# A hybrid decoder step: four queue places on VectorE in an already tuned kernel

## The chip, the core and the metric

The kernel runs on one core of a Trainium2 chip. A core has five engines with a queue of instructions each: TensorE (PE, matrix multiply into PSUM), VectorE (DVE), ScalarE (ACT), GpSimd (POOL) and SyncE (SP). An engine takes its instructions in the order of its queue and waits, where one needs it, on the result of another engine or on a DMA transfer; what is queued behind a waiting instruction waits with it. The metric is the time of one execution on the device in microseconds (us); lower is better.

## The reference, cut

One inference step through two trunk layers of width 1024: 16 meta tokens and 1024 prompt tokens as one sequence, and 8 sequences that decode one token each. Everything is float32.

```python
# layer 0: h += conformer_conv(rmsnorm(h));  h += mlp(rmsnorm(h))
# layer 1: h += rwkv7(rmsnorm(h));           h += mlp(rmsnorm(h));  then a final rmsnorm
def _sqrelu_mlp(h, w_in, w_out):                       # 1024 -> 4096 -> 1024
    return jnp.square(jax.nn.relu(h @ w_in)) @ w_out

def _rwkv7(h, shift_prev, S0, ...):
    prev = concatenate([shift_prev[:, None, :], h[:, :-1]], axis=1)
    xx = prev - h                                      # the token-shift difference
    xr, xw, xk, xv, xa, xg = (h + xx * x_mix[i] for i in range(6))
    r, k, v = xr @ w_r, xk @ w_k, xv @ w_v
    decay = exp(-exp(-softplus(-(w0 + tanh(xw @ w1) @ w2)) - 0.5))
    a = sigmoid(a0 + (xa @ a1) @ a2);  g = sigmoid(xg @ g1) @ g2
    ...
    S_final, ys = lax.scan(_wkv7_step, S0, xs)         # 16 heads, 64 x 64 states
    ...                                                # group norm, bonus
    return ((yn + bonus) * g) @ w_o, h[:, -1], S_final

def _wkv7_step(S, inp):
    sa = einsum('bhvk,bhk->bhv', S, -kk_t)
    S = S * w_t + sa * (kk_t * a_t) + v_t * k_t
    return S, einsum('bhvk,bhk->bhv', S, r_t)
```

## The kernel before, in words

Activations lie with the 1024 channels on the partitions, as 8 tiles of 128 (KT = 8), and tokens along the free side. Each dense product is made of three matmuls of rounded halves (helper lines L190, L191, L192: high by high, high by the weight's low half, low by high). The low halves come from a subtraction at L142 (VectorE, tiles hl, z_l) or L165 (GpSimd, wo_lo, wi_lo), the high ones from a cast on ScalarE (L141, L158). The projections of RWKV (L909) use plain float32.

The MLP runs over 32 blocks of the hidden 4096: `ps_in` is the product into the block, VectorE applies the norm's factor at L347, ScalarE the ReLU at L348, L141 and L142 split it into `hh` and `hl`, and `out` collects the products back, which VectorE adds onto `h` at L360. VectorE's reading of `ps_in` for `hl` frees its PSUM bank.

Layer 0 handles the tokens in three groups (G0). Layer 1 handles them in two ways:

- The projections are made in four groups (G1). `prepare(g)` loads the normed tokens `hx` from DRAM and makes `xx` = previous token minus token, eight subtractions (L873) of which k = 2 and k = 5 go to GpSimd and six to VectorE; group 3 has one more for the 8 decode tokens (L878). `mix` makes the mixed inputs `mx` (L883). For each pair of heads the keyed factors follow: `rk`, `wa` (a scan of the log decays at L1122, then L1141, L1142, L1144), ScalarE's exponentials `em`, `ex`, and the products `ab` at L1153 and L1154.
- The recurrence runs over 17 chunks. Each chunk needs the inverse of a small triangular matrix. `inverses(c, n)` makes them for n chunks at once, five times in all (from chunks 0, 1, 5, 9 and 13): it loads the strictly triangular part `n` into `ni` from DRAM, runs up to 30 pairs of a product `tt` (L1208) and a sum `ni` (L1209) on VectorE, and stores the result, which `chunk` loads as `p` (L1240 transposes it, L1309 makes block copies of it). `nmask` (L774, L775) is the mask by which `n` is cut out of its product; it needs the load `m_ar`. In a chunk, `A` (L1246), `W`, `U`, `S` and `Y` are TensorE's products, `nr` and `xa` VectorE's copies of A, `fs` and `sv` VectorE's update of the state.

The later chunks run as fillers between the steps of the output projection (`mixer_out`, tiles z_h, z_l, ps_oo) and of the MLP of layer 1's first group. `decode_step` does the 8 decode tokens: four TensorE transposes (`pdd`), a store of six vectors to DRAM (`d_dec`), their load by heads (`dq`), then 16 slices of the state with products `t` (L1444), `sa`, `Sdec`, and the result `yd`, stored and reloaded as `eyd`, whose group norm begins with the sum `emsd` (L1469).

What sets the order: the program is written as interleaved generators (each `yield` gives a credit to the next), and a scheduler orders each engine's queue from its own model of durations, except where the source fixes it. In the RWKV part and layer 1 TensorE's order is the order in which it is written (`in_order`). Two calls fix places on other engines: `kept_place(x)` keeps an instruction in the order in which it is written, and

```python
with tc.issue_after(ins):
    ...
```

puts the instructions of its block that run on the engine of `ins` behind `ins` in that queue. It adds no wait of its own. `marks["hl2"][j]` is the split hl of MLP block j of layer 0's last group.

Of the kernel before, what the change touches and what calls it, by code (L numbers as in the profile page):

```python
# [12 lines left out]
ALU = mybir.AluOpType  # L13
# [3 lines left out]
P = 128  # L17
# [17 lines left out]
CHUNKS = [(1, 4), (5, 4), (9, 4), (13, 4)]  # L35
# [11 lines left out]
def hybrid_step(tc, x_prompt, x_sample, state_conv, state_shift, state_wkv, meta_tokens,  # L47
# [10 lines left out]
    with ctx:  # L58
# [715 lines left out]
        nc.vector.tensor_scalar(nmask, m_ar[:, :32], par32[:, 0:1], None, op0=ALU.mult)  # L774
# [59 lines left out]
        prep, norm, kept, scans = {}, {}, {}, {}  # L834
# [22 lines left out]
        def prepare(g):  # L857
# [13 lines left out]
            for k in range(KT):  # L871
                with nullcontext() if g else tc.issue_after(marks["hl2"][k + 5]):
                    first = (nc.gpsimd if k % 3 == 2 else nc.vector).tensor_sub(xx[:, k, :npr], hx[:, k, 0:npr], hx[:, k, 1:1 + npr])  # L873
                if g and k in (0, 2):
                    kept_place(first)
                yield
            if npr < n:
                nc.vector.tensor_sub(xx[:, :, npr:n], sps, hx[:, :, 1 + npr:1 + n])  # L878
# [65 lines left out]
        def mixer_in(g, tick):  # L944
# [140 lines left out]
            for p in range(KT):  # L1085
# [61 lines left out]
                for s in segs:  # L1147
                    e = ex[:, s[4]:s[4] + s[2], :s[3]]
                    e = bass.AP(e.tensor, e.offset, [*e.ap[:2], (1, 2), e.ap[2]])
                    two = lambda t: t[:, :, s[1]:s[1] + s[2] * s[3]].rearrange("p i (c t) -> p c i t", t=s[3])  # L1150
                    out = lambda i: ab[:, s[4]:s[4] + s[2], i:i + 2, :s[3]]

                    nc.vector.tensor_mul(out(0), two(rk2), e)  # L1153
                    nc.vector.tensor_mul(out(2), two(wa[:, :2, :]), cols(em, s).unsqueeze(2).broadcast_to([P, s[2], 2, s[3]]))  # L1154
# [33 lines left out]
        def inverses(c, n):  # L1188
# [8 lines left out]
            group = next((g for g in range(4) if CHUNKS[g][0] > max(c, 1)), None)  # L1197
            while group and group not in scans:
                yield 1
# [3 lines left out]
            for j in range(top - 2, 0, -1):  # L1203
# [3 lines left out]
                with tc.issue_after(scans[group]) if group and j == top - 2 else nullcontext():  # L1207
                    nc.vector.tensor_mul(o, ni[:, :j, j:j + 1].broadcast_to([B, j, wd]), ni[:, j:j + 1, j + 1:top].broadcast_to([B, j, wd]))  # L1208
# [206 lines left out]
        def decode_step():  # L1415

            with ExitStack() as s:
# [12 lines left out]
                yield 6  # L1430
# [149 lines left out]
        with ExitStack() as l1:  # L1580
# [15 lines left out]
            def mixer_out(g, actp, fill, add):  # L1596
# [5 lines left out]
                for p in range(0, KT, per):  # L1602
# [6 lines left out]
                    for i in range(some):  # L1609
                        split(z[0][p + i][:, :n], z[1][p + i][:, :n], v[:, i], nc.vector)  # L1610
# [72 lines left out]
            DL, DN, NL = 74, 90, 16  # L1683
# [75 lines left out]
```

## Time and profile before

| | |
|---|---|
| runs | 2680.71, 2673.79, 2672.78 us |
| median | 2673.79 us |
| profiled execution | 2680.24 us, its span 2678.5 us |
| mean granted TensorE clock | 0.991 |
| busy: TensorE | 2602.9 us (97%) |
| busy: VectorE | 1725.7 us (64%) |
| busy: ScalarE | 1132.7 us (42%) |
| busy: GpSimd | 1450.9 us (54%) |

A row of the timeline gives the start in us from the span's start, the duration in us, the engine, the source line, the operation, output and inputs by name, shapes, and in brackets the idle time of that engine just before it with what ended it. Adjacent instructions of one kind are put together (x8). Buffer numbers are left out of names. A row of a table by stretch gives the stretch, its length, the busy time of TensorE, its weight loads, VectorE, ScalarE and GpSimd with their counts, then the granted clock (1.00 is full speed), the share of the DMA engines and GB/s.

### The profile page before, as it was taken

Reading aid. Unit: us, or ns where it says so; the run is one execution under the profiler, and the core shown is the slowest. Engines: PE = TensorE matmul, PEld = TensorE weight load, DVE = VectorE, ACT = ScalarE, POOL = GpSimd, SP = SyncE. Lnnn points to the kernel's source line nnn. Section 1 sums busy time; section 2 is a strip of 40 time slices with the busy share of each in tenths; the row PEclk is TensorE's granted clock in tenths of the full one; section 3 lists DMA queues with packets and bytes.
Section 4 is the critical chain, followed back from the end, with each engine's and each line's share of the span. In section 5 each row is a group of like instructions: output and inputs, shape, how many; then the busy total and the mean of one; then the engine's idle time right before and its main releaser. Section 6 shows DMA issues by size and latency. Waiting matters only on the chain.

```text
span 2678.5 us, 51360 instructions
## 1 busy us (share of the span) xinstructions
PE 2602.9 (97%) x19796; PEld 2450.6 (91%) x19796; DVE 1725.7 (64%) x3584; ACT 1132.7 (42%) x2097; POOL 1450.9 (54%) x2060
## 2 busy tenths in 40 slices
PE   9999999999999999999899999899999999999998
PEld 8999999999998999877777887689999999999998
DVE  6999999997445444444857567686679643344435
ACT  5546445444444333333344445545443542222223
POOL 7677878878877776122211113375578763333331
PEclk9999999999999999999999999999999999999999
DMA  6663544554456443668766867897666542222211
GB/s 188 176 168 104 167 141 132 158 177 134 142 154 183 124 138 113 201 188 211 188 181 180 206 168 193 209 211 179 156 204 176 155 131 71 64 71 71 67 52 44
DMA packets 602058, 400.20 MB, mean 149 GB/s; under 512 B 96128, under 2 KB 548928, under 8 KB 601814
## 3 DMA queue, kind: packets, MB, share of 16 engines
q1 hardware_dynamic: 573764, 360.08, 49.1%
q0 software_dynamic: 8720, 26.35, 3.1%
q10 hardware_dynamic: 19330, 10.49, 1.4%
q8 instruction: 156, 2.56, 0.4%
q14 instruction: 88, 0.72, 0.1%
HBM read 338.94 MB, written 58.83 MB: 149 GB/s over the span
## 4 chain that ended last, share of the span: by engine, by line
PE 79%; DVE 11%; DMA 3%; ACT 2%; issue 2%; POOL 2%; SPq 0%; ACTq 0%; DVEq 0%; POOLq 0%
PE out L190 8%; PE ps_in L190 8%; PE ps_in L192 8%; PE ps_in L191 8%; PE out L191 8%; PE out L192 8%; PE pk L909 4%; PE pr L909 3%; PE pv L909 2%; DVE tt L1208 1%; DVE ni L1209 1%; PE ps_g L190 1%; PE ps_o L192 1%; PE ps_g L191 1%; PE ps_g L192 1%
## 5 line engine op out<-in xcount | busy, mean ns | idle before, releaser
L165 POOL TENSOR_TENSOR wo_lo<-wo_raw,wo_hi 128x256 fp32r<-128x256 f32 x736 | 539.3, 765 | 290.0 <-ACT wo_hi L158 281.0
L165 POOL TENSOR_TENSOR wi_lo<-wi_raw,wi_hi 128x256 fp32r<-128x256 f32 x640 | 474.7, 774 | 250.5 <-ACT wi_hi L158 249.8
L190 PE MATMUL out<-hh,wo_hi 128*128 128x352 f32 (+2 forms) x1536 | 499.8, 325 | 14.9 <-DVE hl L142 10.2
L360 DVE TENSOR_TENSOR h<-h,out 128x352 f32<-128x352 f32 (+2 forms) x768 | 386.9, 512 | 169.7 <-PE out L192 168.0
L190 PE MATMUL ps_in<-m_h,wi_hi 128*128 128x352 f32 (+2 forms) x1536 | 495.3, 322 | 0.0
L192 PE MATMUL ps_in<-m_l,wi_hi 128*128 128x352 f32 (+2 forms) x1536 | 494.2, 322 | 1.1 <-DVE m_l L288 1.1
L191 PE MATMUL out<-hh,wo_lo 128*128 128x352 f32 (+2 forms) x1536 | 494.5, 322 | 0.0
L191 PE MATMUL ps_in<-m_h,wi_lo 128*128 128x352 f32 (+2 forms) x1536 | 492.9, 321 | 0.0
L192 PE MATMUL out<-hl,wo_hi 128*128 128x352 f32 (+2 forms) x1536 | 492.8, 321 | 0.0
L542 DVE SCALAR_TENSOR_TENSOR cv<-u,wdw,cv 128x348 f32<-128x348 f32 (+2 forms) x720 | 378.4, 577 | 0.7
L158 ACT CAST wi_hi<-wi_raw 128x1024 fp32r<-128x1024 f32 x160 | 167.6, 1049 | 398.1 <-PE out L192 199.0
L158 ACT CAST wo_hi<-wo_raw 128x1024 fp32r<-128x1024 f32 x184 | 192.7, 1048 | 318.3 <-PE out L192 169.9
L190 PEld LDWEIGHTS out<-hh,wo_hi 128*128 128x128 f32 x1536 | 291.0, 189 | 21.1 <-DVE hl L142 11.5
L192 PEld LDWEIGHTS ps_in<-m_l,wi_hi 128*128 128x128 f32 x1536 | 289.2, 188 | 2.6 <-DVE m_l L288 2.1
L190 PEld LDWEIGHTS ps_in<-m_h,wi_hi 128*128 128x128 f32 x1536 | 290.3, 189 | 1.4
L191 PEld LDWEIGHTS out<-hh,wo_lo 128*128 128x128 f32 x1536 | 290.1, 189 | 0.8
L191 PEld LDWEIGHTS ps_in<-m_h,wi_lo 128*128 128x128 f32 x1536 | 289.5, 188 | 0.6
L192 PEld LDWEIGHTS out<-hl,wo_hi 128*128 128x128 f32 x1536 | 289.8, 189 | 0.0
L347 DVE SCALAR_TENSOR_TENSOR ps_in<-ps_in,rs_m 128x352 f32<-128x352 f32 (+2 forms) x192 | 100.6, 525 | 258.1 <-PE ps_in L192 257.8
L142 DVE TENSOR_TENSOR hl<-ps_in,hh 128x352 fp32r<-128x352 f32 (+2 forms) x192 | 98.7, 515 | 125.2 <-ACT hh L141 125.2
L1074 POOL DMA_DIRECT2D d_n<-n x32 | 24.3, 760 | 217.5 <-DVE n L1064 112.4
L348 ACT ACTIVATE ps_in<-ps_in 128x352 f32<-128x352 f32 (+2 forms) x192 | 85.1, 444 | 125.2 <-DVE ps_in L347 124.8
(367 smaller groups left out, 4770.1 us busy)
## 6 DMA issues: line engine op xcount, KB each, us to landing
wi_raw<-in_w_mlp_in_dram SPq DMA_DIRECT2D x160, 512.0 KB
wo_raw<-in_w_mlp_out_dram SPq DMA_DIRECT2D x160, 512.0 KB
wk_raw<-in_rwkv_w_k_dram SPq DMA_DIRECT2D x32, 512.0 KB
wr_raw<-in_rwkv_w_r_dram SPq DMA_DIRECT2D x32, 512.0 KB
wv_raw<-in_rwkv_w_v_dram SPq DMA_DIRECT2D x32, 512.0 KB
d_ab<-ab POOLq DMA_DIRECT2D x32, 512.0 KB, 4.5
pg_raw<-in_conv_w_pw_dram SPq DMA_DIRECT2D x24, 512.0 KB
pa_raw<-in_conv_w_pw_dram SPq DMA_DIRECT2D x24, 512.0 KB
```

What stands on the lines that cost most here:

```text
L142: return eng_lo.tensor_sub(lo, src, hi.bitcast(F32))
L158: cast = nc.scalar.copy(hi[:, :a * b], raw[:, :a * b])
L165: eng_lo.tensor_sub(lo[:, cs], raw[:, cs], hi[:, cs].bitcast(F32))
L190: nc.tensor.matmul(ps, w[0], act[0], start=first, stop=False)
L191: nc.tensor.matmul(ps, w[1], act[0], start=False, stop=False)
L192: nc.tensor.matmul(ps, w[0], act[1], start=False, stop=last)
L347: nc.vector.scalar_tensor_tensor(s, s, 0.0, rs()[:, :n], op0=ALU.max, op1=ALU.mult)
L348: nc.scalar.activation(s, s, AF.Square)
L360: total = nc.vector.tensor_add(hv[:, 4 * i + m, :], hv[:, 4 * i + m, :], ps[:, :n])
L542: nc.vector.scalar_tensor_tensor(acc[m][:, :n], ug[:, m, j:j + n], wdw[:, m, j:j + 1], acc[m][:, :n], op0=ALU.mult, op1=ALU.add)
L909: nc.tensor.matmul(ps[:, :n], w[:, k, :], act[k], start=k == 0, stop=k == KT - 1)
L1208: nc.vector.tensor_mul(o, ni[:, :j, j:j + 1].broadcast_to([B, j, wd]), ni[:, j:j + 1, j + 1:top].broadcast_to([B, j, wd]))
```

## The change

Four edits, all about the order of queues:

1. The first operation of `nmask` is placed behind the split hl of MLP block 14 of layer 0's last group.
2. The differences `xx` of groups 1, 2 and 3 (and the decode's in group 3) are placed behind the first keyed product of the group before (`decayed`, L1154); the two `kept_place` are dropped.
3. The first product `tt` of the last inverse (chunks 13 to 16) is placed behind the last split `z_l` of `mixer_out(0)` (`scans[4]`); the other inverses had such a place already.
4. `decode_step` gives up its turn for 12 credits instead of 6 after the load of `dq`, and its share of the fillers grows from 90 to 96.

```diff
-        nc.vector.tensor_scalar(nmask, m_ar[:, :32], par32[:, 0:1], None, op0=ALU.mult)
+        with tc.issue_after(marks["hl2"][14]):
+            nc.vector.tensor_scalar(nmask, m_ar[:, :32], par32[:, 0:1], None, op0=ALU.mult)
...
-        prep, norm, kept, scans = {}, {}, {}, {}
+        prep, norm, kept, scans, decayed = {}, {}, {}, {}, {}
...
             for k in range(KT):
-                with nullcontext() if g else tc.issue_after(marks["hl2"][k + 5]):
-                    first = (nc.gpsimd if k % 3 == 2 else nc.vector).tensor_sub(xx[:, k, :npr], hx[:, k, 0:npr], hx[:, k, 1:1 + npr])
-                if g and k in (0, 2):
-                    kept_place(first)
+                with tc.issue_after(decayed[g - 1] if g else marks["hl2"][k + 5]):
+                    (nc.gpsimd if k % 3 == 2 else nc.vector).tensor_sub(xx[:, k, :npr], hx[:, k, 0:npr], hx[:, k, 1:1 + npr])
                 yield
             if npr < n:
-                nc.vector.tensor_sub(xx[:, :, npr:n], sps, hx[:, :, 1 + npr:1 + n])
+                with tc.issue_after(decayed[g - 1]):
+                    nc.vector.tensor_sub(xx[:, :, npr:n], sps, hx[:, :, 1 + npr:1 + n])
...
-                    nc.vector.tensor_mul(out(2), two(wa[:, :2, :]), cols(em, s).unsqueeze(2).broadcast_to([P, s[2], 2, s[3]]))
+                    keyed = nc.vector.tensor_mul(out(2), two(wa[:, :2, :]), cols(em, s).unsqueeze(2).broadcast_to([P, s[2], 2, s[3]]))
+                decayed.setdefault(g, keyed.ins)
...
-            group = next((g for g in range(4) if CHUNKS[g][0] > max(c, 1)), None)
-            while group and group not in scans:
+            group = next((g for g in range(4) if CHUNKS[g][0] > max(c, 1)), 4)
+            while group not in scans:
                 yield 1
...
-                with tc.issue_after(scans[group]) if group and j == top - 2 else nullcontext():
+                with tc.issue_after(scans[group]) if j == top - 2 else nullcontext():
...
-                yield 6
+                yield 12
...
-                        split(z[0][p + i][:, :n], z[1][p + i][:, :n], v[:, i], nc.vector)
+                        low = split(z[0][p + i][:, :n], z[1][p + i][:, :n], v[:, i], nc.vector)
+                scans.setdefault(4, low.ins)
...
-            DL, DN, NL = 74, 90, 16
+            DL, DN, NL = 74, 96, 16
```

No engine gets an instruction more or less; the scheduler makes a new order around the four places, on all five engines. Line numbers of the changed kernel are one or two higher in this part. Three places on VectorE are shown, each before and after.

First, VectorE around the second inverse, in the projections of group 1 and group 2. The tt and ni rows are the end of the pairs, p (L1309, L1310 after) the block copies made of the finished inverse, rk, wa, ab the factors of the head pair in hand. Before:

```order
L1209 TENSOR_TENSOR ni_13990<-ni_13990,tt_1_14353 128x30
L1122 SCALAR_TENSOR_TENSOR wa_4_14487<-smask_13609,wa_4_14487 128x256
L1141 TENSOR_TENSOR wa_4_14487<-st_4_13342,wa_4_14487 128x256
L1064 TENSOR_TENSOR n_3_14531<-nn_3_14532,nmask 128x128
L1080 TENSOR_TENSOR bv_3_14553<-vv_3_14360,pk_3_14551 128x256
L1144 SCALAR_TENSOR_TENSOR rk_4_14569<-rk_4_14480,pvec,wa_4_14487 128x256
L1121 SCALAR_TENSOR_TENSOR rk_4_14480<-st_4_13342,negs,pb_4_14555 128x256
L1142 TENSOR_TENSOR wa_4_14487<-rk_4_14480,wa_4_14487 128x256
L1153 TENSOR_TENSOR ab_4_14571<-rk_4_14480,ex_4_14562 128x4x128
L1154 TENSOR_TENSOR ab_4_14571<-wa_4_14487,em_4_14560 128x4x128
L1240 STREAM_TRANSPOSE x_14590<-p_14517 128x256
L1309 TENSOR_SCALAR p_14680<-p_14517,par32q 128x8x32 x2
```

After:

```order
L1122 SCALAR_TENSOR_TENSOR wa_4_14487<-smask_13609,wa_4_14487 128x256
L1141 TENSOR_TENSOR wa_4_14487<-st_4_13342,wa_4_14487 128x256
L1064 TENSOR_TENSOR n_3_14531<-nn_3_14532,nmask 128x128
L1310 TENSOR_SCALAR p_14680<-p_14517,par32q 128x8x32 x2
L1080 TENSOR_TENSOR bv_3_14553<-vv_3_14360,pk_3_14551 128x256
L1144 SCALAR_TENSOR_TENSOR rk_4_14569<-rk_4_14480,pvec,wa_4_14487 128x256
L1121 SCALAR_TENSOR_TENSOR rk_4_14480<-st_4_13342,negs,pb_4_14555 128x256
L1142 TENSOR_TENSOR wa_4_14487<-rk_4_14480,wa_4_14487 128x256
L1153 TENSOR_TENSOR ab_4_14571<-rk_4_14480,ex_4_14562 128x4x128
L1154 TENSOR_TENSOR ab_4_14571<-wa_4_14487,em_4_14560 128x4x128
L1241 STREAM_TRANSPOSE x_14590<-p_14517 128x256
```

The block copies of p, which need the load of the inverse, moved ahead of bv, both rk, wa and the two ab.

Second, VectorE at the first steps of the last inverse, where mixer_out(0) splits its input into z_l. Before:

```order
L1080 TENSOR_TENSOR bv_7_19212<-vv_7_19032,pk_7_19210 128x264
L142 TENSOR_TENSOR z_l_19255<-zr_19263,z_h_19247 128x328
L142 TENSOR_TENSOR z_l_19256<-zr_19263,z_h_19248 128x328
L142 TENSOR_TENSOR z_l_19257<-zr_19263,z_h_19249 128x328
L1208 TENSOR_TENSOR tt_19385<-ni_19215 128x30
L142 TENSOR_TENSOR z_l_19258<-zr_19280,z_h_19250 128x328
L142 TENSOR_TENSOR z_l_19259<-zr_19280,z_h_19251 128x328
L1209 TENSOR_TENSOR ni_19215<-ni_19215,tt_19385 128x30
```

After:

```order
L142 TENSOR_TENSOR z_l_19261<-zr_19288,z_h_19253 128x328
L142 TENSOR_TENSOR z_l_19262<-zr_19288,z_h_19254 128x328
L1209 TENSOR_TENSOR tt_19385<-ni_19215 128x30
L1210 TENSOR_TENSOR ni_19215<-ni_19215,tt_19385 128x30
L1209 TENSOR_TENSOR tt_19385<-ni_19215 128x58
L1210 TENSOR_TENSOR ni_19215<-ni_19215,tt_19385 128x29x2
L1209 TENSOR_TENSOR tt_19385<-ni_19215 128x84
L1210 TENSOR_TENSOR ni_19215<-ni_19215,tt_19385 128x28x3
L1365 TENSOR_TENSOR fs_19381<-S_19325,wc 128x512
```

The first tt moved from behind the third z_l to behind the eighth; fs of the running chunk now follows the third pair, where before it followed the fifth tt.

Third, VectorE around the decode's first product t, in the MLP of layer 1's first group. Before:

```order
L347 SCALAR_TENSOR_TENSOR ps_in_16_0_22368<-ps_in_16_0_22368,rs_m_20041 128x328
L142 TENSOR_TENSOR hl_16_22367<-ps_in_16_0_22368,hh_16_22366 128x328
L1497 TENSOR_TENSOR ebv_1_22325<-ez_1_22356,ebv_1_22325 128x512
L1498 TENSOR_TENSOR egt_1_22326<-ebv_1_22325,egt_1_22326 128x512
L347 SCALAR_TENSOR_TENSOR ps_in_17_0_22418<-ps_in_17_0_22418,rs_m_20041 128x328
L360 TENSOR_TENSOR h_0_19245<-h_0_19245,out_7_0_0_22457 128x328
L360 TENSOR_TENSOR h_0_19245<-h_0_19245,out_7_0_1_22465 128x328
L1444 TENSOR_TENSOR t_22559<-Sdec_22558,dq 128x256
L142 TENSOR_TENSOR hl_16_22367<-ps_in_17_0_22418,hh_16_22366 128x328
```

After:

```order
L360 TENSOR_TENSOR h_0_19245<-h_0_19245,out_6_0_6_22335 128x328
L360 TENSOR_TENSOR h_0_19245<-h_0_19245,out_6_0_7_22349 128x328
L347 SCALAR_TENSOR_TENSOR ps_in_16_0_22374<-ps_in_16_0_22374,rs_m_20041 128x328
L1445 TENSOR_TENSOR t_22630<-Sdec_22629,dq 128x256
L142 TENSOR_TENSOR hl_16_22373<-ps_in_16_0_22374,hh_16_22372 128x328
L1498 TENSOR_TENSOR ebv_1_22331<-ez_1_22362,ebv_1_22331 128x512
```

The product t moved from ahead of the hl of block 17 to ahead of the hl of block 16. Four more moves belong to these edits: the pair that makes nmask went from between the evacuation (L347) and the hl of MLP block 5 to right behind the hl of block 14, ahead of the evacuation of block 15; the last of the decode's transposes on TensorE went 34 instructions forward; the rk copy and wa of group 2's second head pair went ahead of the square (L1472) of the chunk's group norm on ScalarE; and near the end of the decode, emsd went from behind the first h of the block pair 28 and 29 to ahead of the hl of block 30.

## The prediction

> **What bounds the kernel now.** I read the page first, then the waits of TensorE, then the timeline around each wait that the change touches, and last tables by stretch of 4 us for the clock.
>
> ```profile
> span 2678.5 us, 51360 instructions
> PE 2602.9 (97%) x19796; PEld 2450.6 (91%) x19796; DVE 1725.7 (64%) x3584; ACT 1132.7 (42%) x2097; POOL 1450.9 (54%) x2060
> ```
>
> TensorE (PE) is busy 97% of the span; 75.6 us are idle. VectorE (DVE) is busy 64%, so moving its work matters only where TensorE waits for it. The change adds and removes no instruction: on all five engines the same instructions stand in another order. So the gain can only be idle time of TensorE, and the slow clock behind idle time. The waits of TensorE say how much idle time each place holds. Columns: engine, tile and line that waited, what it waited for, sum in us, times, longest.
>
> ```profile
> PE out L190 <- DVE hl L142: 10.2, 5, 5.4
> PE ps_oo L192 <- DVE z_l L142: 5.8, 2, 5.2
> PE l_a L1108 <- DVE rk L1121: 5.8, 1, 5.8
> PE pv L909 <- ACT rk L1089: 3.6, 3, 2.7
> PE A L1246 <- DVE fs L1364: 2.6, 2, 1.6
> PE pk L1078 <- ACT vv L1114: 2.0, 1, 2.0
> ```
>
> Each of the longest waits in these rows lies beside an instruction that the change moves. That is 5.4 + 5.2 + 5.8 + 2.7 + 1.6 + 2.0 = 22.7 us, an upper bound on idle time removed, before clocks. I go through them in order of time.
>
> **1. The norm mask (nmask).** VectorE first, then GpSimd (POOL), TensorE, and the clock afterwards.
>
> ```profile
> 863.63 3.64 DVE L774 TENSOR_SCALAR nmask<-m_ar,par32q 128x32 f32<-128x32 f32 x1 [4.22 <-DMA m_ar<-m_ar]
> 867.47 0.51 DVE L142 TENSOR_TENSOR hl<-ps_in,hh 128x348 fp32r<-128x348 f32 x1
> 861.69 5.54 POOL L165 TENSOR_TENSOR wo_lo<-wo_raw,wo_hi 128x256 fp32r<-128x256 f32 x8
> 868.03 0.66 PE L190 MATMUL out<-hh,wo_hi 128*128 128x348 f32 x1 [5.40 <-DVE hl L142]
> 868.00:872.00 4.00, 3.96 (x15) 3.97 (x16) 2.69 (x7) 0.00 (x0) 0.00 (x0) 0.54 0.48 138
> ```
>
> VectorE stands 4.22 us for the load of m_ar, then the product takes 3.64 us, and the residual split hl of the MLP, which frees a PSUM bank, is queued behind it. TensorE stands 5.40 us. In the next 4 us the granted clock (the third number from the end) is 0.54, so 0.46 x 4 = 1.8 us more are lost. Together 7.2 us. In the changed order the pair stands between the hl of MLP block 14 and the evacuation of block 15, some 75 us on, when m_ar has landed. The rows there, before the change:
>
> ```profile
> 940.37 0.52 DVE L142 TENSOR_TENSOR hl<-ps_in,hh 128x348 fp32r<-128x348 f32 x1 [1.43 <-ACT hh L141]
> 942.21 0.53 DVE L347 SCALAR_TENSOR_TENSOR ps_in<-ps_in,rs_m 128x348 f32<-128x348 f32 x1 [1.32 <-PE ps_in L192]
> 939.58 2.83 POOL L165 TENSOR_TENSOR wi_lo<-wi_raw,wi_hi 128x256 fp32r<-128x256 f32 x4 [0.97 <-ACT wi_hi L158]
> ```
>
> There 1.32 us are idle. The 3.64 us product ended within 0.04 us of the end of GpSimd's run of eight (861.69 + 5.54 = 867.23). If it is held in that way again, it ends at 939.58 + 2.83 = 942.41, and with the second product (0.25) the evacuation starts near 942.7 instead of 942.21, 0.5 us late. At worst it takes 3.64 us again: 940.89 + 3.64 + 0.25 = 944.78, 2.6 us late. I take **-7.2**, range -7.2 to -4.6, since a shift of 0.5 us is hidden as long as TensorE has not used up its free banks. The page "SBUF — State Buffer" of the Trainium skill (section "SBUF: two separate sides") says that a VectorE instruction in a 2-port mode and a GpSimd instruction exclude each other for the whole instruction; the ends in the rows agree with this, and by it the new place would be held once more, which costs the 0.5 us and not 3.64.
>
> **2. Differences xx of groups 1 to 3.** Their six subtractions stand at DMA-fed places in VectorE's queue; now they follow the previous group's first keyed product (L1154).
>
> Group 1:
>
> ```profile
> 1145.56 0.72 DVE L1122 TENSOR_TENSOR_SCAN wa<-smask,wa 128x272 f32<-128x272 f32 x1
> 1147.71 0.91 PE L1078 MATMUL pk<-rk,hsum 128*128 128x272 f32 x2 [1.99 <-ACT vv L1114]
> 1148.87 4.93 PE L909 MATMUL pk<-mx,wk_raw 128*128 128x256 f32 x16
> 1148.00:1152.00 4.00, 4.00 (x13) 3.26 (x13) 2.78 (x7) 0.07 (x1) 1.84 (x5) 0.57 0.45 114
> 1330.88 3.72 PE L909 MATMUL pv<-mx,wv_raw 128*128 128x256 f32 x16
> ```
>
> The scan of the decays waits behind the xx and the mixes; ScalarE waits for the scan, and TensorE 1.99 us for ScalarE. The 16 matmuls after it took 4.93 us, against 3.72 at full clock: 1.2 more. At most 3.2 us. The changed order puts the wait for the load off VectorE's path, and the scan comes some 1.5 us sooner, which leaves about 0.4 of the wait: **-2.8**, range -3.2 to 0. The page "TensorE: Matmul & The Clock Gate" (section "Part 1: The HAM clock gate (the "warmup" mystery)") has the clock fall after an idle window of about 3.4 us; here 0.57 was granted after a wait of 1.99 us, so the measurement decides. By the page's rule this place would be worth 2.0 and not 3.2 us at most.
>
> Group 2:
>
> ```profile
> 1273.62 0.42 DVE L873 TENSOR_TENSOR xx<-hx 128x256 f32<-128x256 f32 x1 [7.90 <-DMA hx<-d_hn]
> 1278.24 5.19 PE L909 MATMUL pv<-mx,wv_raw 128*128 128x256 f32 x16
> 1335.88 0.42 DVE L1080 TENSOR_TENSOR bv<-vv,pk 128x256 f32<-128x256 f32 x1 [0.30 <-PE pk L1078]
> 1336.63 0.48 DVE L1121 SCALAR_TENSOR_TENSOR rk<-st,negs,pb 128x256 f32<-128x256 f32 x1
> 1337.48 0.68 DVE L1153 TENSOR_TENSOR ab<-rk,ex 128x512 f32<-128x512 f32 x1
> 1343.86 0.45 DVE L1240 STREAM_TRANSPOSE x<-p 128x256 f32<-128x256 f32 x1 [5.09 <-DMA p<-d_p]
> 1345.85 1.13 PE L1246 MATMUL A<-xa,bk 64*128 64x128 f32 x14 [1.04 <-DVE nr L1256]
> ```
>
> VectorE stands 7.90 us for hx with rk (L1121) behind it, which frees the bank that l_a needs: 5.81 us of TensorE, plus 5.19 - 3.72 = 1.5 of clock, 7.3 in all. But the second chunk's inverse arrives by a DMA that VectorE awaits until 1343.86, and TensorE waits for the nr made of it. That chain of 30 pairs and three transfers is not sped up by TensorE coming earlier. It gains only what VectorE no longer stands in front of it, and TensorE would meet the same inverse again. Also, the block products of p for that chunk (L1309) now stand ahead of bv, rk, rk2, wa and the two ab of one of group 1's head pairs (by the rows, 0.42 for bv and wa, 0.48 for each rk, 0.68 for each ab: 3.2 us); before they stood behind. So nr comes up to 3.2 us later after the landing. If VectorE's 7.90 us of waiting bring the chain 4.6 us forward, nr is 1.4 us sooner, and TensorE with it: **-1.4**. That 4.6 is my choice between nothing and 7.9, a little above the middle, because the pairs fill VectorE alone. Best case -7.3; worst case, with the landing unmoved, +3.2 and 1.5 for the clock, +4.7.
>
> Group 3: the waits of A for fs (1.6) and of pv for ScalarE's rk (2.7) have their rows above. The changed order of ScalarE has rk ahead of the square that awaits VectorE, but fs now comes behind the xx. I take somewhat over half of 4.3: **-2.5**, range -4.3 to 0.
>
> **3. The last inverse's first step (tt, ni).**
>
> ```profile
> 1741.90 0.21 DVE L1208 TENSOR_TENSOR tt<-ni 128x30 f32<-128x30 f32 x1 [4.80 <-DMA ni<-d_n]
> 1742.02 2.01 DVE L142 TENSOR_TENSOR z_l<-zr,z_h 128x328 fp32r<-128x328 f32 x2
> 1743.14 0.64 PE L192 MATMUL ps_oo<-z_l,wo_hi 128*128 128x328 f32 x1 [5.19 <-DVE z_l L142]
> 1744.00:1748.00 4.00, 4.00 (x80) 4.00 (x79) 3.83 (x13) 0.00 (x0) 0.62 (x1) 0.50 1.05 325
> 1750.07 0.42 PE L190 MATMUL ps_oo<-z_h,wo_hi 128*128 128x328 f32 x1
> ```
>
> VectorE stands 4.80 us for ni with five of eight z_l splits behind it; TensorE stands 5.19, and 0.50 of clock for 4 us costs 2.0. At most 7.2. Now all z_l come first. But fs of the running chunk (which frees the bank that the next A needs) stands behind three pairs of the inverse, and these start no sooner than 1741.90: six steps of about 0.2 to 0.25 and their gaps are 1.5, fs 0.7, so A starts at 1744.1 and, at the full clock, ps_oo resumes 1.2 later, near 1745.3 to 1745.6 against 1750.07: **-4.5**, range -7.2 to 0.
>
> **4. The decode's query product (t, dq).**
>
> ```profile
> 1965.93 0.51 DVE L347 SCALAR_TENSOR_TENSOR ps_in<-ps_in,rs_m 128x328 f32<-128x328 f32 x1 [3.55 <-PE ps_in L192]
> 1968.14 0.50 DVE L142 TENSOR_TENSOR hl<-ps_in,hh 128x328 fp32r<-128x328 f32 x1 [1.70 <-ACT hh L141]
> 1976.07 0.63 DVE L1444 TENSOR_TENSOR t<-Sdec,dq 128x256 f32<-128x256 f32 x1 [3.92 <-DMA dq<-d_dec]
> 1977.15 0.42 PE L190 MATMUL out<-hh,wo_hi 128*128 128x328 f32 x1 [2.91 <-DVE hl L142]
> ```
>
> The transposes before the load move 34 TensorE instructions earlier; at 2602.9 / 19796 = 0.13 us that is about 4.5 us, so dq lands near 1971.5. But t moves too: from behind the evacuation of block 17 to right behind that of block 16 (the row of 1965.93), ahead of hl of block 16. There it would wait about 5 us (from 1966.44), and hl comes at 1972.1 and not at 1968.14, 4.0 us late. The wait is moved, not removed: **-0.5**. Range -2.9 (all of the old wait) to +2.9 (TensorE sees the 4.0 and 1.8 of clock, and no longer the 2.91).
>
> **5. The decode's tail.** This is where the changed pace costs something.
>
> ```profile
> 2078.10 0.42 DVE L1452 TENSOR_REDUCE yd<-t 128x4 f32<-128x256 f32 x1
> 2081.35 0.48 DVE L142 TENSOR_TENSOR hl<-ps_in,hh 128x328 fp32r<-128x328 f32 x1
> 2083.52 0.67 DVE L1469 TENSOR_REDUCE emsd<-eyd 8x8 f32<-8x512 f32 x1
> ```
>
> The sum emsd needs yd by two transfers, and stands now ahead of hl of block 30, which came 2.2 us before it. The first load and the store ahead of it are issued sooner, so I take **+1.5**; range 0 to +4.9 (hl behind 2083.52 + 0.67 is 2.9 late, and 2 of clock).
>
> **The sum.** -7.2 - 2.8 - 1.4 - 2.5 - 4.5 - 0.5 + 1.5 = -17.4. The profiled execution took 2680.24 us (span 2678.5 and 1.7 around it), 6.45 over the median of 2673.79. So 2680.24 - 17.4 = 2662.8 in its terms, and 2656.4 at the median. 0.3%, about what a measurement of this kernel can tell from no change, is 8.0 us.
>
> **The rivals.**
>
> *All waits go (0.15).* The loads hx, ni and dq have landed when their users come up, and the inverse chain keeps up: -7.2 - 3.2 - 7.3 - 4.3 - 7.2 - 0.5 + 0 = -29.7, 2644 us. For it: the waits are for transfers that are independent of the work behind them. Against: the 5.09 us wait for p at 1343.86 and the fs behind the pairs.
>
> *The waits are handed on (0.17).* In the recurrence VectorE and the transfers set the pace, so every early start ends in front of the next inverse, and edit 4 does not do what it says, since t and its load move together. What is left is the mask, 2 us of the z_l place and the tail: -7.2 - 2 + 1.5 = -7.7, 2666 us. For it: the chain of section 2. Against: groups 1 and 3 have no awaited inverse in their rows.
>
> *Slower: VectorE held at DMA-fed instructions with bank-freeing work behind them (0.08).* The new order puts p ahead of rk and ab (+4.7), t ahead of hl (+2.9) and emsd ahead of hl (+4.9); the mask is held its full 3.64 us again (-4.6), and xx and z_l gain nothing: +7.9, 2681.7 us. It decides from the point where the holds together cost TensorE more than the 4.6 us that the mask still gives. For it: the 3.92 us wait for dq. Against: it needs all three at their worst.
>
> **How the numbers follow.** The forecast of section 1 to 5 has 0.60. Its own ends overlap the second rival. The range 2644 to 2669 takes in the first rival's value, the second's, and leaves out about 0.2. Faster by over 0.3% means under 2665.8: nearly all of the forecast (0.56), all of the first rival (0.15), a third of the second (0.06): 0.77. Slower means over 2681.8: 0.07. Within: 0.16.
>
> **What would show it.** Right: TensorE's wait of 5.40 for hl is gone and the clock stays near 1 in the stretch after it; l_a no longer waits for rk; ps_oo no longer waits for z_l, with A waiting about 2 us for fs instead; VectorE's wait for dq is still 3 to 5 us, at a block earlier; a wait of VectorE for eyd is new. The step on group 2 is right if the wait for p comes back 4 to 5 us earlier and most of 7.3 us is lost by A. The prediction is wrong if waits of TensorE for rk, bv or nr over 4 us appear near the second chunk, or if the mask is held at its new place with TensorE behind it.

## The result and the profile after

The changed kernel takes 2656.68 us (median of 4 runs, 2654.59 to 2657.72); the kernel before, run beside it, 2676.97 us (4 runs, 2672.78 to 2680.71). The ratio is 0.9924, 95% interval 0.9904 to 0.9944. Measured a second time, the pair gave 2660.83 (4 runs) and 2674.92 us (7 runs), ratio 0.9951 (0.9936 to 0.9965). The profiled execution took 2656.18 us with a span of 2654.4 us, 24.1 us under the span of before. The page's head, after:

```profile
span 2654.4 us, 51355 instructions
PE 2594.9 (98%) x19796; PEld 2445.4 (92%) x19796; DVE 1719.6 (65%) x3584; ACT 1132.9 (43%) x2097; POOL 1453.9 (55%) x2060
```

TensorE's idle time fell from 75.6 to 59.5 us, 16.1 us; its busy time fell by 8.0 us with the same 19796 matmuls. The mean granted clock rose from 0.991 to 0.994, and 0.003 of the span is about those 8.0 us: clock that is no longer lost behind the waits. What TensorE waits for now, from the view of its waits (sum, times, longest):

```profile
PE pb L804 <- ACT vv L1114: 11.3, 7, 5.3
PE out L190 <- DVE h L360: 7.6, 6, 2.0
PE A L1247 <- DVE fs L1365: 3.6, 2, 3.4
PE pv L909 <- ACT rk L1089: 0.9, 2, 0.7
PE pk L1078 <- ACT vv L1114: 0.9, 1, 0.9
PE out L190 <- DVE hl L142: 1.3, 2, 0.9
```

The waits of 5.4 (hl), 5.8 (l_a for rk) and 5.2 us (ps_oo for z_l) are gone from their places. Two new ones stand near: pb for vv, 5.3, and A for fs, 3.4; before, these two pairs had no wait longer than 1.7 and 1.6 us.

TensorE's order is fixed in the RWKV part, so the same instruction can be found in both traces and its start compared. This gives the gain by place. Each number is the change, over that stretch, of (start after less start before). The last column is the same for the trace of the second measurement (run f_again, span 2659.2 us):

| stretch, us of before | what was moved there | forecast | measured | second trace |
|---|---|---|---|---|
| up to 862 | nothing | 0 | +0.4 | +1.6 |
| 862 to 873 | mask | -7.2 | -7.3 | -7.3 |
| 1136 to 1157 | xx, group 1 | -2.8 | -2.6 | -2.6 |
| 1157 to 1428 | xx, group 2 | -1.4 | -6.5 | -5.4 |
| 1428 to 1473 | xx, group 3 | -2.5 | -1.2 | -1.2 |
| 1473 to 1733 | nothing | 0 | -0.9 | -0.4 |
| 1733 to 1787 | last inverse | -4.5 | -2.8 | -1.5 |
| 1787 to 1840 | nothing | 0 | -2.1 | -1.2 |
| 1840 to 2072 | query product | -0.5 | -2.1 | -0.2 |
| 2072 to 2089 | the decode's tail | +1.5 | +1.3 | -0.7 |
| to the end | nothing | 0 | -0.3 | -0.3 |
| sum | | -17.4 | -24.1 | -19.2 |

Both columns are taken against the one trace of before. Its execution (2680.24 us) is among the slowest of that kernel, so what it lost by chance stands in both columns as a gain.

One instruction as an example, the first matmul of the MLP block behind the mask, in TensorE's timeline of before and then of the changed kernel: 6.9 us apart, and 0.4 the other way ahead of the mask.

```profile
873.58 0.32 PE L190 MATMUL ps_in<-m_h,wi_hi 128*128 128x348 f32 x1
```

```profile
866.69 0.32 PE L190 MATMUL ps_in<-m_h,wi_hi 128*128 128x348 f32 x1
```

### The profile page after: what moved, and what is told of

Read it like the earlier page. It is cut to its first block, busy times and chain, and to the rows that moved or that the text cites. A ratio compares the mean times of both kernels' runs of the same rounds, so it can differ in the third digit from the quotient of the medians.

```text
span 2654.4 us, 51355 instructions
## 1 busy us (share of the span) xinstructions
PE 2594.9 (98%) x19796; PEld 2445.4 (92%) x19796; DVE 1719.6 (65%) x3584; ACT 1132.9 (43%) x2097; POOL 1453.9 (55%) x2060
## 4 chain that ended last, share of the span: by engine, by line
PE 83%; DVE 9%; ACT 2%; DMA 2%; issue 2%; POOL 1%; ACTq 0%; SPq 0%; DVEq 0%; POOLq 0%
PE ps_in L190 8%; PE ps_in L192 8%; PE ps_in L191 8%; PE out L190 8%; PE out L191 8%; PE out L192 8%; PE pk L909 4%; PE pr L909 4%; PE pv L909 2%; PE ps_g L190 1%; PE ps_o L192 1%; PE ps_g L191 1%; PE ps_g L192 1%; PE ps_o L190 1%; PE ps_o L191 1%
## 5 line engine op out<-in xcount | busy, mean ns | idle before, releaser
L347 DVE SCALAR_TENSOR_TENSOR ps_in<-ps_in,rs_m 128x352 f32<-128x352 f32 (+2 forms) x192 | 100.7, 525 | 256.4 <-PE ps_in L192 256.1
```

Source lines behind the costliest of these rows:

```text
L347: nc.vector.scalar_tensor_tensor(s, s, 0.0, rs()[:, :n], op0=ALU.max, op1=ALU.mult)
```

## The experiments

Each kernel ran beside the kernel before on the same chip; three chips were used, one for each batch, and the changed kernel itself ran on only one of these three. Runs of different batches are compared by their ratios to the kernel before. A trace of another execution of the same order differs at places by 1 to 4 us, so a gain of one stretch is called shown only where several traces agree.

**The four edits one by one.** The diffs are those of the change, one edit at a time: the mask (edit 1), the differences (edit 2), the last inverse (edit 3), the decode (edit 4).

> The norm mask's edit alone. Theory (each edit pays at its own place): TensorE's 5.40 us wait for hl and the slow clock behind it go, and every later place stands 6.9 us earlier and stays so: the time falls by 7 us (6 to 8). Rival (the gains hang together: a place that starts earlier only pays because the places behind it were cleared too): part of the 6.9 us is given back at the next awaited load in the recurrence, and the time falls by 2 to 4 us. In both theories the mask's two operations take under 1 us together at the new place.

> The differences' edit alone. Theory (own place): group 1 gives 2.6, group 2 gives 8.5, loses 7.7 again to a new wait of pb for ScalarE, and wins 4 to 6 more by the earlier second inverse, group 3 gives 1: 10 to 12 us in all, of which the first half of the recurrence shows 9. Rival (chance alignment): with the recurrence at the old distance from the layer before, waits of 1 us each at the second inverse do not go, and the time falls by 4 to 6 us.

> The last inverse's edit alone. Theory (own place): the 5.19 us wait of ps_oo for z_l is replaced by a wait of A for fs of 3 to 4 us, and 2 us of clock are won later: the time falls by 2 to 5 us. Rival (the gain in this stretch came from the earlier recurrence): 0 to 1 us.

> The decode's edit alone. Theory (own place): the query product still waits 2 to 4 us for its load, the wait of TensorE of 2.91 us for hl shrinks to about 2 for h, and 1.3 us are lost in the tail: the time falls by 0 to 2 us. Rival (the changed pace is what matters: the decode's work shares the MLP differently): the stretch up to the tail gains 2 us and the tail loses nothing, 2 to 4 us.

| edit alone | median, us | before there, us | ratio (95%) |
|---|---|---|---|
| mask | 2671.79 | 2677.82 | 0.9983 (0.9974 to 0.9993) |
| differences | 2664.98 | 2677.82 | 0.9954 (0.9940 to 0.9969) |
| last inverse | 2671.95 | 2677.82 | 0.9981 (0.9970 to 0.9992) |
| decode | 2674.55 | 2677.82 | 0.9987 (0.9977 to 0.9997) |

Each edit alone is faster, by 0.1 to 0.5%. The differences are worth most: 12.8 us by the medians, 10 to 12 expected. The mask gives 6.0, the lower end of its theory's 6 to 8. The last inverse gives 5.9, more than the 2 to 5 expected, while its own stretch gives 3.0 in its trace; the rest is not explained. The product of the four ratios is 0.9905, inside the interval of the first comparison and below that of the second: the medians add to 28.0 us, and the four together gave 20.3 and 14.1. That an edit paid only because another had cleared the way isn't borne out; that part of a gain is lost when the four stand together is likely, but not settled by these intervals. The decode's 3.3 us at the median is at the upper side of what its rival expected (2 to 4), and its trace shows 0.8 us lost and not gained between 1840 and 2089, so this edit is not explained by its own run.

These four kernels hold more than their own edit: three of them have the mask at its old place, in the same order. VectorE's row of the mask's first product in each, and TensorE's wait behind it. With the differences' edit:

```profile
863.93 0.76 DVE L774 TENSOR_SCALAR nmask<-m_ar,par32q 128x32 f32<-128x32 f32 x1 [4.43 <-DMA m_ar<-m_ar]
865.87 0.42 PE L190 MATMUL out<-hh,wo_hi 128*128 128x348 f32 x1 [3.14 <-DVE hl L142]
```

With the last inverse's edit:

```profile
864.31 0.35 DVE L774 TENSOR_SCALAR nmask<-m_ar,par32q 128x32 f32<-128x32 f32 x1 [3.81 <-DMA m_ar<-m_ar]
865.43 0.43 PE L190 MATMUL out<-hh,wo_hi 128*128 128x348 f32 x1 [1.70 <-DVE hl L142]
```

With the decode's edit, and GpSimd's run beside it:

```profile
862.40 0.36 DVE L774 TENSOR_SCALAR nmask<-m_ar,par32q 128x32 f32<-128x32 f32 x1 [3.75 <-DMA m_ar<-m_ar]
859.91 2.81 POOL L165 TENSOR_TENSOR wo_lo<-wo_raw,wo_hi 128x256 fp32r<-128x256 f32 x4
863.53 0.42 PE L190 MATMUL out<-hh,wo_hi 128*128 128x348 f32 x1 [1.64 <-DVE hl L142]
```

The 3.64 us of before is no property of the instruction: here it took 0.35 to 0.76 us, and TensorE waited 1.64 to 3.14 us and not 5.40. So the trace from which the mask's -7.2 was worked out holds one of the long waits, which these three executions did not have.

**The mask and the decode undone in the changed kernel, and the changed kernel once more.**

> The changed kernel once more, as it is, for a second trace on the chip of the next three. Both theories: the same time as first measured against before, 20 us less (ratio 0.992), with a spread of 3 us or less over its runs.

> The changed kernel with the norm mask's edit undone. Theory A (the 3.64 us of the mask's first product in the trace of before was bad luck: it lost the port to GpSimd five times in a row, which other executions of the same order do not): TensorE's wait for hl is 1.6 to 3.2 us in this trace, and the kernel is 3 to 5 us slower than the changed one, with a spread over its runs larger than the changed kernel's. Theory B (the wait is 5.4 us in nearly every execution): 7 us slower and no larger spread.

> The changed kernel with the decode's edit undone. Theory (the wait for the load only moves with the product): 0 to 2 us slower than the changed kernel. Rival (the edit is worth what its own run showed at the median, 3.3 us): 3 to 4 us slower.

The edits undone:

```diff
-        with tc.issue_after(marks["hl2"][14]):
-            nc.vector.tensor_scalar(nmask, m_ar[:, :32], par32[:, 0:1], None, op0=ALU.mult)
+        nc.vector.tensor_scalar(nmask, m_ar[:, :32], par32[:, 0:1], None, op0=ALU.mult)
```

```diff
-                yield 12
+                yield 6
-            DL, DN, NL = 74, 96, 16
+            DL, DN, NL = 74, 90, 16
```

All three on one chip, with before at 2674.92 us: the changed kernel 2660.83 us (2660.26 to 2661.44, as narrow as expected, though the gain is 14 and not 20 us), without the mask's edit 2661.50 (2659.53 to 2663.06), without the decode's edit 2659.21 (2657.28 to 2665.05). By these medians neither edit is told from nothing: 0.7 us slower without the mask's, where both theories expected 3 us or more, and 1.6 us faster without the decode's, where 0 to 2 or 3 to 4 us slower was expected. In the trace without the mask's edit the long hold was back, with GpSimd's run ending 0.03 us before it:

```profile
865.74 3.33 DVE L774 TENSOR_SCALAR nmask<-m_ar,par32q 128x32 f32<-128x32 f32 x1 [4.27 <-DMA m_ar<-m_ar]
863.52 5.52 POOL L165 TENSOR_TENSOR wo_lo<-wo_raw,wo_hi 128x256 fp32r<-128x256 f32 x8
869.84 0.66 PE L190 MATMUL out<-hh,wo_hi 128*128 128x348 f32 x1 [5.14 <-DVE hl L142]
```

That execution (2663.06 us) is the slowest of its four. In five traces of the old place TensorE's wait is 5.40, 5.14, 3.14, 1.70 and 1.64 us; the mask's edit is worth 7.3 us against the worst of them and about 2 against the best. Neither theory holds whole. Theory A expected 1.6 to 3.2 us for this trace and 5.14 came; theory B expected the long wait nearly always, and three traces of five are shorter. So the wait differs from one execution to the next, and by these five the long one is no rare case. The larger spread that theory A expected is there (3.5 against 1.2 us, four runs each). The trace without the decode's edit shows the old wait of TensorE back, by name and size (2.91 before):

```profile
1956.33 0.64 PE L190 MATMUL out<-hh,wo_hi 128*128 128x328 f32 x1 [3.23 <-DVE hl L142]
```

**Group 2 of the differences put back.**

> The changed kernel with the differences of group 2 put back as before (groups 1 and 3 as changed). Theory (group 2 pays through the inverse chain, which starts earlier by the whole wait): TensorE's wait of l_a for rk of 5.8 us and the waits of 1 us each of gg for x, pb for vv and A for nr behind the second inverse come back, and the wait of pb of 5.3 to 6.0 us goes: 4 to 7 us slower than the changed kernel. Rival (the prediction's sum, the wait is handed on): 1.4 us slower.

```diff
-                with tc.issue_after(decayed[g - 1] if g else marks["hl2"][k + 5]):
-                    (nc.gpsimd if k % 3 == 2 else nc.vector).tensor_sub(...)
+                with nullcontext() if g == 2 else tc.issue_after(decayed[g - 1] if g else marks["hl2"][k + 5]):
+                    first = (nc.gpsimd if k % 3 == 2 else nc.vector).tensor_sub(...)
+                if g == 2 and k in (0, 2):
+                    kept_place(first)
```

2664.14 us (2661.18 to 2665.13), before on that chip 2676.16, ratio 0.9952 (0.9937 to 0.9966). TensorE's timeline:

```profile
1269.27 1.22 PE L1110 MATMUL l_a<-lwa,wa 64*128 64x256 f32 x2 [5.76 <-DVE rk L1123]
1311.14 0.38 PE L804 MATMUL pb<-r16h,hspread 128*128 128x256 f32 x1 [0.90 <-ACT vv L1116]
1337.55 1.13 PE L1249 MATMUL A<-xa,bk 64*128 64x128 f32 x14 [1.07 <-DVE nr L1259]
```

As the theory had it, the wait of l_a and the small ones behind it (pb, A) are back, and that of pb for vv is gone. Against the changed kernel's trace TensorE loses 4.7 us between 1250 and 1332, and 1.7 of them come back at group 3. The traces on record narrow it further. From 1310 to 1350 us of before, five that have this edit (the changed kernel twice, e2_xx, g_state_first, f_undecode) gain 3.2 to 3.3 us each, and four that don't (e1_mask, e3_inverse, e4_decode, this one) gain nothing. So group 2's place is worth 3 to 5 us, not 1.4, and not the whole 6.5 that the first pair of traces shows: 1.1 of these is a wait of gg for x that was gone in three of the four without the edit too. The run times don't settle it: 0.9952 against 0.9924 and 0.9951 for the changed kernel.

**The differences behind the next scan.** The new wait of pb in the changed kernel has a plain cause in its trace: VectorE, ScalarE, then TensorE.

```profile
1262.66 2.94 DVE L874 TENSOR_TENSOR xx<-hx 128x256 f32<-128x256 f32 x6 [4.39 <-DMA hx<-d_hn]
1268.93 0.67 DVE L1122 TENSOR_TENSOR_SCAN wa<-smask,wa 128x256 f32<-128x256 f32 x1
1269.63 0.42 ACT L1125 ACTIVATE em<-wa 128x256 f32<-128x256 f32 x1 [6.56 <-DVE wa L1122]
1270.66 0.58 PE L804 MATMUL pb<-r16h,hspread 128*128 128x256 f32 x1 [5.29 <-ACT vv L1114]
1271.26 5.48 PE L909 MATMUL pk<-mx,wk_raw 128*128 128x256 f32 x16
```

VectorE waits 4.39 us for hx again, now with the second pair's scan behind the xx and mixes; ScalarE's em, ex and vv wait for the scan and TensorE for vv. The next kernel puts the xx of all groups behind that pair's km, which follows its scan:

> The changed kernel with the differences of groups 1 to 3 placed behind km of the previous group's second head pair, that is behind that pair's scan, and not behind the first pair's keyed product. Theory (the new wait of pb for vv of 5.3 to 6.0 us is the scan, queued behind differences and mixes that wait for hx): this wait goes, the key product behind it waits 1 to 2 us for the mixes instead, the waits of 0.9 and 2.0 us in groups 1 and 3 shrink: 4 to 8 us faster than the changed kernel. Rival (TensorE needs the mixes of hx at the same time, so the load sets the pace whatever the order): 0 to 2 us, with a wait of pk for mx of 4 us or more.

```diff
-                nc.vector.tensor_mul(km[:, :n], kp[:, :n], am[:, :n])
+                made = nc.vector.tensor_mul(km[:, :n], kp[:, :n], am[:, :n])
+                if p == 1 and g < 3:
+                    decayed[g] = made.ins
+                    for _ in coming:
+                        pass
+                    ks = carry["keys"] = keys(g + 1, both)
+                    next(ks)
...
-                decayed.setdefault(g, keyed.ins)
```

2653.84 us (2652.62 to 2657.89), ratio 0.9919 (0.9902 to 0.9936), the lowest median of all. TensorE's order is the same; its wait at that place, with VectorE's mix before it:

```profile
1267.55 0.47 DVE L883 SCALAR_TENSOR_TENSOR mx<-xx,pvec,hx 128x256 f32<-128x256 f32 x1
1268.11 6.74 PE L909 MATMUL pk<-mx,wk_raw 128*128 128x256 f32 x16 [2.46 <-issue]
```

The wait of pb is gone and pk waits 2.46 us instead, at a key product that needs the mixes of hx itself. The profile names no releaser for this wait; VectorE's first mix ends at 1268.02, just before it is over. So both theories hold in part: the order cost something, the load sets the rest. In groups 1 and 3 the waits did not shrink as expected: pk now waits 1.2 us in group 1, pb 2.2 in group 3, and pv waits 1.6 us for rk again. Against the changed kernel's trace TensorE is level at 1250, 1.9 us ahead at 1281, 4.5 ahead at 1443, and 1.3 ahead at 1601: part of it is given back. Its interval overlaps those of the changed kernel in both measurements (0.9924, 0.9951), so that it is faster than the changed kernel isn't settled; both beat the kernel before.

**The last inverse placed further back.** In the changed kernel z_l runs through, and the wait stands in front of fs:

```profile
1717.23 3.36 DVE L142 TENSOR_TENSOR z_l<-zr,z_h 128x328 fp32r<-128x328 f32 x8
1723.26 0.72 DVE L1209 TENSOR_TENSOR tt<-ni 128x30 f32<-128x30 f32 x1 [2.66 <-DMA ni<-d_n]
1725.60 0.68 DVE L1365 TENSOR_TENSOR fs<-S,wc 128x512 f32<-128x512 f32 x1
1726.34 2.07 PE L1247 MATMUL A<-xa,bk 64*128 64x128 f32 x14 [3.44 <-DVE fs L1365]
1728.00:1732.00 4.00, 4.00 (x15) 3.77 (x15) 3.85 (x10) 0.51 (x2) 2.22 (x2) 0.50 1.13 305
```

Two kernels take that away: the first tt behind fs of chunk 10, and behind the last nr of chunk 11.

> The changed kernel with the last inverse's first product placed behind the state update fs of chunk 10, not behind the last z_l. Theory (the wait of A for fs is the old wait of ps_oo in a new place): A's wait of 3.44 us and about 2 us of slow clock behind it go: 4 to 6 us faster than the changed kernel. Rival (the last inverse is needed that early, so what fs gains is lost at chunk 13): no faster, with a new wait of TensorE for nr or x near chunk 13.

```diff
+            if c == 10:
+                scans[4] = state.ins
...
-                scans.setdefault(4, low.ins)
```

> The changed kernel with the last inverse's first product placed behind the last nr of chunk 11. Theory (whatever frees a bank behind the awaited load is waited for next: z_l before, fs after, nr with fs first): no wait of TensorE over 2 us remains in that stretch, 3 to 6 us faster than the changed kernel. Rival (the last inverse becomes late for chunk 13): a new wait of TensorE for gg, nr or x near chunk 13 of 2 us or more, no gain.

```diff
+                if c == 11 and j:
+                    scans[4] = copied.ins
...
-                scans.setdefault(4, low.ins)
```

(state and copied are the instructions of fs and nr.) Behind fs: 2656.22 us (2653.66 to 2662.15), 4.6 under the changed kernel on its chip, but with a spread of 8.5 that takes in all of the changed kernel's runs. Its trace has A's wait gone and this one in its place:

```profile
1736.13 1.94 PE L1316 MATMUL bT<-ident,bk 128*128 128x128 f32 x8 [3.49 <-DVE nr L1257]
```

Behind nr: 2658.45 us (2656.26 to 2661.65), ratio 0.9934 (0.9918 to 0.9949), between the two of the changed kernel; the 3 to 6 us expected are not shown. No wait over 2 us is left there, as expected, but 20 us later TensorE meets a load:

```profile
1753.43 0.46 PE L1247 MATMUL A<-xa,bk 64*128 64x128 f32 x2 [1.04 <-issue]
1754.69 1.74 PE L1247 MATMUL A<-xa,bk 64*128 64x128 f32 x14 [0.81 <-DMA bk<-d_ab]
```

By the same TensorE instructions the two traces are 4.4 and 4.9 us behind the changed kernel's at 1715 (from other places), 2.0 ahead and 0.7 behind at 1734, and 4.5 and 4.3 behind again at 1766: against this trace, what was won is given back within 32 us. The second trace of the changed kernel, where nothing was moved, does the same (2.6 behind, 0.2, 4.1) and meets the same load. Against that one, behind fs keeps 1.4 us of what it won and behind nr 2.1. So whether the two moves gain anything stays open; that the load of bk is the next limit is seen in two traces.

**Both moves in one kernel.**

> Both of the two moves (behind km of the second head pair, behind nr of chunk 11) in one kernel. Theory (the two places are apart): the two gains add, 7 to 13 us faster than the changed kernel. Rival (the second half of the recurrence is paced by the inverses, so an earlier start there is given back): no more than the larger of the two.

2658.73 us (2655.69 to 2660.05), ratio 0.9931 (0.9916 to 0.9946): the gains don't add. TensorE, which came early, waits for the values of the next chunk:

```profile
1737.92 0.30 PE L1325 MATMUL W<-sv,xa 128*64 128x64 f32 x2 [3.21 <-DMA sv<-d_v]
```

The time is what the rival expected, no more than the larger of the two gains. But the wait in this trace is for the load of the chunk's values, not for an inverse as the rival had it; that the loads pace the whole stretch is not shown by one trace.

## Why the prediction was right, step by step

The forecast was 2656.4 us, the measured median 2656.68. Part of this closeness is chance: the traces of the two kernels are 24.1 us apart, not 17.4, the medians 20.3 in one measurement and 14.1 in the other, and terms erred in both directions. Where a term agrees with the first trace, the second trace often differs, so the table's last column is needed to read it.

- **The bound.** TensorE's idle time and the clock behind it were the whole gain: 16.1 us of idle time and 8.0 of busy time. For the mask the tables by stretch priced the clock well: -7.2 forecast, -7.3 in the two traces.
- **The mask.** The mechanism was right. The size rests on one execution: 3.64 us of its 7.2 were a hold that three of five traces of the old place lack. At the new place the rows are these, with GpSimd's beside them:

```profile
933.92 0.25 DVE L775 TENSOR_SCALAR nmask<-m_ar,par32q 128x32 f32<-128x32 f32 x1
934.20 0.67 DVE L776 SCALAR_TENSOR_TENSOR nmask<-m_ar,par32q,nmask 128x32 f32<-128x32 f32 x1
932.69 2.83 POOL L165 TENSOR_TENSOR wi_lo<-wi_raw,wi_hi 128x256 fp32r<-128x256 f32 x4 [0.98 <-ACT wi_hi L158]
935.32 0.53 DVE L347 SCALAR_TENSOR_TENSOR ps_in<-ps_in,rs_m 128x348 f32<-128x348 f32 x1 [0.45 <-PE ps_in L192]
```

  Nothing is late: the evacuation waits 0.45 us for TensorE. The 0.5 us that the prediction allowed for was not spent. In the run times the edit is worth 6.0 us alone and 0.7 when it is undone.
- **Group 1.** -2.8 forecast, -2.6 measured, and -2.6 to -2.7 in the seven further traces with this edit as it stands; the remaining wait of 0.9 us, where 0.4 was forecast, is the row of pk in the waits. The wait shrank by 1.1 us; the rest is clock, 1.00 in the 4 us behind it where it had been 0.57. The old place is less steady: without the edit the stretch differs from before by 0.0, -1.6 and +1.5.
- **Group 2: the step that was mis-sized** is "that 4.6 is my choice between nothing and 7.9". The copies of p were awaited here until

```profile
1323.75 0.62 DVE L1310 TENSOR_SCALAR p<-p,par32q 128x256 f32<-128x256 f32 x2 [2.14 <-DMA p<-d_p]
```

  that is 20.1 us before the 1343.86 of before, 10.6 more than the 9.5 us that TensorE had gained up to group 1. So the chain came forward by more than VectorE's wait, and the A behind it no longer waits. The first product of this inverse, before and after:

```profile
1300.40 0.21 DVE L1208 TENSOR_TENSOR tt<-ni 128x30 f32<-128x30 f32 x1 [3.52 <-DMA ni<-d_n]
```

```profile
1283.41 0.20 DVE L1209 TENSOR_TENSOR tt<-ni 128x30 f32<-128x30 f32 x1 [2.44 <-DMA ni<-d_n]
```

  It starts 17.0 us earlier, 7.5 more than TensorE's lead, so nearly all of the 7.9 and not 4.6 reached the inverse. Its 30 pairs then took 31.0 us from the first product to the last sum, where they had taken 33.8. With group 2 put back they took 33.8 again. The chain of waits that the prediction followed had a second hole. It saw rk freed from behind xx, but not that the next pair's scan stands behind the same xx. That gave the new wait of 5.3 us, nearly as long as the old one of 5.8. Most of the gain came only afterwards: the waits of pb (0.9) and of A for nr (1.0) are gone, 3.2 to 3.3 us with what lies around them.
- **Group 3.** -2.5 forecast, -1.2 in the two traces of the changed kernel, but -2.9 in five others with the same edit there, so the size was about right. pv's 2.7 us and fs's 1.6 went; pb's wait rose from 1.5 to 2.0, and bT now waits 1.3 for nr. The -0.9 behind it isn't explained; the second trace has -0.4 there.
- **The last inverse.** Mechanism right: z_l free, A waits for fs until 1726.34, which is 17.8 us before the 1744.1 that the prediction gave, against a lead of 18.1. What was missed in this trace is the clock: the new wait of 3.44 us is followed by 4 us at 0.50, 2 us that are about the 1.7 by which -2.8 falls short of -4.5. The second trace shows that the clock is not all. There A waits 1.96 us, as the prediction said, the clock behind it stays at 1.00 (behind group 1's wait of 1.99 us it was 0.57, so the length of the wait alone doesn't decide), and yet the stretch gives only -1.5. Between 1734 and 1766 TensorE falls 3.9 us back against the first trace, where it meets the load of bk (TensorE's rows, then the clock behind the first):

```profile
1729.25 1.16 PE L1247 MATMUL A<-xa,bk 64*128 64x128 f32 x14 [1.96 <-DVE fs L1365]
1754.49 1.55 PE L1247 MATMUL A<-xa,bk 64*128 64x128 f32 x14 [1.01 <-DMA bk<-d_ab]
1728.00:1732.00 4.00, 2.75 (x25) 2.63 (x26) 3.80 (x10) 0.51 (x2) 1.82 (x3) 1.00 1.04 337
```

  The edit alone gives -3.0 in the same stretch, and the kernels without it between -0.1 and +0.6. The further -2.1 up to 1840 is not the edit's: kernels without it show 1.6 to 3.4 there too.
- **The query product.** The load moved and the product with it, as forecast, but the load came forward further:

```profile
1945.90 0.87 DVE L1445 TENSOR_TENSOR t<-Sdec,dq 128x256 f32<-128x256 f32 x1 [2.20 <-DMA dq<-d_dec]
1946.68 0.49 DVE L142 TENSOR_TENSOR hl<-ps_in,hh 128x328 fp32r<-128x328 f32 x1
1951.49 0.42 PE L190 MATMUL out<-hh,wo_hi 128*128 128x328 f32 x1 [1.99 <-DVE h L360]
```

  It is 30.2 us earlier than 1976.07 where TensorE is 23.0 earlier: 7.2, not 4.5. VectorE waits 2.20, not 5 us, and TensorE 1.99 for h, not 2.91 for hl. The -2.1 of this stretch is not shown to be the edit's: the second trace has -0.2 and the edit alone +1.0. Whether the edit pays in the runs stays open: alone it is 3.3 us faster, and the changed kernel without it was 1.6 us faster, too.
- **The tail: right by chance.** +1.5 forecast and +1.3 in this trace, but -0.7 in the second trace of the same kernel. The mechanism did not show. The row of emsd has no wait for eyd; it stands ahead of hl behind the four z_l that stood there before, and takes 0.67 us:

```profile
2055.88 0.67 DVE L1470 TENSOR_REDUCE emsd<-eyd 8x8 f32<-8x512 f32 x1
2056.48 0.48 DVE L142 TENSOR_TENSOR hl<-ps_in,hh 128x328 fp32r<-128x328 f32 x1
```

  TensorE waits 0.92 us for this hl, and 0.91 in the second trace. What sets the two apart is the wait for h behind it, first in this trace, then in the second:

```profile
2059.62 0.42 PE L190 MATMUL out<-hh,wo_hi 128*128 128x328 f32 x1 [1.44 <-DVE h L360]
```

```profile
2065.58 0.42 PE L190 MATMUL out<-hh,wo_hi 128*128 128x328 f32 x1 [0.51 <-DVE h L360]
```

The rivals: not all waits went (z_l's and l_a's came back under other names), and they were not merely handed on, since the second inverse came early enough. At the last inverse they were handed on in part, and the gain of 14.1 us of the second measurement lies between the forecast's 17.4 and the 7.7 of that rival. The slower one needed p, t and emsd to hold VectorE; p held it 2.14 and t 2.20 us, emsd not at all.

## What to carry to other kernels

When an instruction that waits for a transfer stands in front of work that frees PSUM banks, putting it behind that work paid here for the differences, in the run times, and for the last inverse in the traces. But go on down the queue, since whatever stands behind its new place (here a scan, fs, then nr) is the next to wait, and behind that the next load. A wait that is priced from one execution should be looked at in a second trace of the same order first, and so should a gain: here the tail changed its sign from one trace to the next. Runs of other kernels that leave the place alone serve as that.

## What the hardware showed unexpectedly

A product of VectorE over 128 x 32 took 0.24 to 0.25 us in each trace with the mask's edit and 0.35, 0.36, 0.76, 3.33 and 3.64 us at the old place. In all these traces it ends within 0.05 us behind the end of one of GpSimd's subtractions; the two long ones ended 0.03 and 0.04 us after the end of a whole run of eight. The Trainium skill, page "SBUF — State Buffer" (section "SBUF: two separate sides"), says that a VectorE instruction in a 2-port mode, or with two inputs in SBUF, and a GpSimd instruction exclude each other for the whole instruction of the one that starts first. The traces agree with that for the short holds (a GpSimd instruction takes 0.7 us); whether this product runs in such a mode they don't show. But 3.33 and 3.64 us are about five of these instructions in a row, so VectorE did not get the next turn. Why, these traces don't show.
